# First shift and scale columns in two loads, tiles 0 and 1 one by one, small inputs on ScalarE's queue

## The chip, the cores and the metric

The kernel runs on one core of a Trainium2 chip. The metric is the device time of one execution in microseconds (us); lower is better. Before the change it is 2581.41 us, the median of three runs.

## What is computed

One layer of a backbone with gated recurrences, for 512 latent tokens x and 256 context tokens, model width D = 2048, all in fp32. The part that matters here is its beginning:

```
mod   = silu(c) @ w_mod + b_mod           # mod_c: the same with c_ctx
sh1, sc1, ... = split(mod, 6)
h  = rmsnorm(x, g_norm1)   * (1 + sc1)  + sh1
hc = rmsnorm(ctx, g_norm1) * (1 + csc1) + csh1
z  = h @ w_in                             # likewise hc @ w_in: the heads' inputs
```

`rmsnorm` divides by the root of the mean square over the 2048 channels, so no h exists before all of x has been seen. The scans, the output projection, the feed-forward part and the final norm follow; the change leaves them as they are.

## The kernel before

x stands transposed, channels on partitions, as 16 channel tiles `xl0` to `xl15` of 128 channels by 512 tokens. ctx stands as `xc`, 16 tiles of 128 by 256. Tiles go in pairs: pair kp is tiles 2kp and 2kp + 1.

**The sum of squares.** `stream_rstd` (called with "l" for latent, "c" for context) squares each tile on ScalarE (ACT), adds it on VectorE (DVE) into one tile `sq_l` or `sq_c`, and sums over the partitions with a product on TensorE (PE) against ones, `ss_l` or `ss_c`. `mean_rsqrt` makes 1/sqrt of it: Ln and Exp on ScalarE, and one Newton step on DVE; the result is `rstd`.

**The columns.** Scale (region 1) and shift (region 0) of a channel tile are columns `scol` and `shcol`. `mod_load` loads four 512 KB pieces of w_mod for one region and one pair; `mod_rows` multiplies them with the activated c and c_ctx (16 products of 256 columns, in the trace 32 records, output `ps_m`) and copies the result on ScalarE (`rows_m`); `mod_cols` turns the rows with two small products into columns, which DVE reads with the bias (`scol`, `shcol`). In the text m1_2 is the scale group of pair 2, m0_1 the shift group of pair 1. These groups and the sums of squares share two PSUM banks in turn ("psb").

**Modulation.** `modulate(n, ...)` multiplies the pair's tiles by rstd, applies the columns on DVE, casts to a high part `hTh` on ScalarE and subtracts on DVE to get a low part `hTl` (`hch`, `hcl` for ctx). Weights are split the same way (`hi_h`, `lo_h`, by `load_split`), and each product is made of three: high x high, high x low, low x high.

**Projection of the first two heads.** `project_first` works along the channel pairs. Head 0 keeps six banks a0_0 to a0_5 in PSUM over all pairs (g = 0, 1: 512 columns; 2, 3: 256 columns; 4, 5: the context, 384 columns). Head 1 has too few banks left: its groups a1_kp_g are made pair by pair (`early_group`), and ScalarE or DVE adds them to sums in SBUF (`e0_g`). The products of pair 0 begin with head 1's first two banks (`early_pair`).

**What sets the order.** While `pinned` is set, PE takes its instructions in the order in which they are written; ScalarE and DVE have a static order from the scheduler, in which `high_priority` moves instructions ahead. All large loads go through SyncE's queue (SP) in the order written. In the trace PE's products read `out<-in` with L95 as their line, since a helper records them all; `a` stands for all banks of both heads.

Of the kernel before, what the change touches and what calls it, by code (L numbers as in the profile page):

```python
# [11 lines left out]
F32 = mybir.dt.float32  # L12
# [57 lines left out]
def block_kernel(ctx: ExitStack, tc: tile.TileContext, a: dict, out: bass.AP):  # L70
# [14 lines left out]
    def add(o, x, y):  # L85
        V.tensor_tensor(out=o, in0=x, in1=y, op=ALU.add)  # L86

    def split(hi, lo, x):
        S.copy(hi, x)  # L89
        return V.tensor_tensor(out=lo, in0=x, in1=hi.bitcast(F32), op=ALU.subtract).ins  # L90
# [66 lines left out]
    fillers = []  # L157
    rate, credit = [0], [0]

    def load_split(src, name, n=2, w=512):  # L160
        raw = wraw.tile([P, n, w], F32, name=f"raw_{name}", tag="raw")
        hi = whi.tile([P, n, w], F32R, name=f"hi_{name}", tag="hi")
        lo = wlo.tile([P, n, w], F32R, name=f"lo_{name}", tag="lo")
        nc.sync.dma_start(raw, src)
        with tc.high_priority():
            split(hi, lo, raw)
# [55 lines left out]

    def mod_rows(region, n, raws):

        bank = psb(f"ps_m{region}_{n}")
        ps = bank[:, 0:256]
# [4 lines left out]
        rows = tmp.tile([P, 256], F32, name=f"rows_m{region}_{n}", tag="rows")  # L231
        with tc.high_priority():
            S.copy(rows, ps)
        return bank, rows

    def mod_cols(region, n, bank, rows):
# [4 lines left out]
        with tc.high_priority():  # L241
            for b in range(2):
                k = 2 * n + b
                if region == 1:
                    V.tensor_scalar(out=scol[:, k, :], in0=pc[:, b, :], scalar1=bp1[:, k : k + 1],
                                    scalar2=gn1[:, k : k + 1], op0=ALU.add, op1=ALU.mult)
                else:
                    V.tensor_scalar(out=shcol[:, k, :], in0=pc[:, b, :], scalar1=bmod[:, k : k + 1],
                                    scalar2=None, op0=ALU.add)

# [51 lines left out]

    def project_chunk(kp, wh, wl, o, g, first=0, last=KT - 1):

        ks = list(enumerate((2 * kp, 2 * kp + 1)))
        if g < 2:
# [39 lines left out]

    def early_pair(w, sums):

        (wh, wl), ps = w, [psb(f"a1_0_{g}", BANKS[g]) for g in range(2)]
        for n, (ws, xs) in enumerate(((wh, hx[0]), (wl, hx[0]), (wh, hx[1]))):  # L350
            for k in range(2):
                for g in range(2):
                    mm(ps[g], ws[:, k, P * g : P * g + P], xs[k], start=(n == 0 and k == 0), stop=(n == 2 and k == 1))
        for g in range(2):
            sums[g] = actp.tile(list(BANKS[g]), F32, name=f"e0_{g}", tag=f"ah{KT - 4 + g}")
            with tc.high_priority():
                S.activation(sums[g], ps[g], AF.Copy, scale=SCALE if g == 0 else 1.0)

    def project_first():

        banks = [acc(f"a0_{g}", BANKS[g]) for g in range(6)]
        sums = [None] * 4 + [accp.tile([P, DK + DV], F32, name=f"e0_{4 + j}", tag=f"sum{j}") for j in range(CJ)]
        stream_rstd(xl, rl, "l", T)
# [3 lines left out]
        for j in range(KT // 2):  # L367
            nc.sync.dma_start(xcp[j], a["ctxT"][j])
        raws = {r: mod_load(r, 1) for r in (1, 0)}
        with tc.high_priority():  # L370
            ins = modulate(0, "x")
# [10 lines left out]
        with tc.high_priority(), tc.issue_after(ins):  # L382
# [10 lines left out]
        w1 = load_split(a["w_heads"][1, 1], f"h1_1")  # L393
        for r in (1, 0):
            raws[r] = mod_load(r, 2)
        nc.sync.dma_start(cst[:, 0:C_SA], a["consts"][:, 0:C_SA])
        project_chunk(0, *w0, banks[4], 4)
        rows = mod_rows(1, 2, raws[1])
        project_chunk(0, *w0, banks[5], 5)
        mod_cols(1, 2, *rows)  # L400
        for kp in range(1, KP):
            for g in range(6):
                if g == 5 and kp + 1 < KP:
                    rows = mod_rows(0, kp + 1, raws[0])
                ins = early_group(kp, g, w1, sums)
                if g == 2:
                    with tc.issue_after(ins):
                        w0 = load_split(a["w_heads"][0, kp], f"h0_{kp}")
                    if kp + 2 < KP:
                        raws[1] = mod_load(1, kp + 2)  # L410
            if kp + 1 < KP:
                mod_cols(0, kp + 1, *rows)
                with tc.issue_after(ins):
                    modulate(kp + 1, "xc")
            for g in range(6):
                if g == 3 and kp + 2 < KP:
# [788 lines left out]
def arrange(x, c, ctx, c_ctx, w_mod, b_mod, g_norm1, g_norm2, w_in, gla_w_lr, gla_b_lr, mlstm_b_gate,  # L1205
# [61 lines left out]
```

## Time and profile before

| | before |
|---|---|
| median of three runs | 2581.41 us (2580.79 to 2584.02) |
| profiled execution, its own time | 2580.88 us |
| its span, first to last instruction | 2579.2 us |
| PE busy | 2536.5 us, 98% of the span |
| DVE busy | 1399.1 us, 54% |
| ACT busy | 789.9 us, 31% |
| first projection product starts | 30.70 us |

The profile is of one execution. Times in the views count from the first instruction. A timeline row gives start, duration, engine, line and operation, and in square brackets the idle time of its engine ahead of it with what ended it. Products overlap a little, so a row's duration is longer than the distance to the next start. PEclk is TensorE's granted clock as a share of 2.4 GHz.

### The profile page before, as it was taken

The numbers are of one execution on the slowest core, as the hardware profiler recorded it, in microseconds if no ns is written. First come the engines' busy times: TensorE is split into PE (matmuls) and PEld (weight loads), VectorE is DVE, ScalarE is ACT, GpSimd is POOL, SyncE is SP. The second block draws the span as 40 slices with busy tenths as digits, with TensorE's granted clock in tenths as the row PEclk, the third lists the DMA queues.
The fourth block names the chain that finished last, engine by engine and source line by source line (L and its number), as shares of the span: only waits on it lengthen the run. The fifth ranks groups of instructions, "written<-read, shape, count | busy, mean of one in ns | idle before, by whom it ended". The sixth has DMA issues, their size and how long they took to land.

```text
span 2579.2 us, 31641 instructions
## 1 busy us (share of the span) xinstructions
PE 2536.5 (98%) x12944; PEld 2128.3 (83%) x12944; DVE 1399.1 (54%) x2071; ACT 789.9 (31%) x1177; POOL 28.2 (1%) x53
## 2 busy tenths in 40 slices
PE   6999999999999999999999999999999999999998
PEld 4887899888887888888888888888888888888887
DVE  6556755554445677449866336533653265336534
ACT  4224543322223233224323123312331233123332
POOL 0000000000000000000000000000000000000001
PEclk9999999999999999999999999999999999999999
DMA  9740011132334777424722222322232223222323
GB/s 383 270 160 34 33 42 50 42 123 99 115 115 165 259 254 238 147 87 159 269 98 91 97 98 98 98 98 94 94 98 98 98 98 97 94 95 89 104 94 107
DMA packets 96345, 321.35 MB, mean 125 GB/s; under 512 B 10884, under 2 KB 15304, under 8 KB 96200
## 3 DMA queue, kind: packets, MB, share of 16 engines
q1 hardware_dynamic: 95112, 318.29, 35.7%
q8 instruction: 101, 1.65, 0.3%
q10 hardware_dynamic: 1088, 1.05, 0.1%
q14 instruction: 44, 0.36, 0.0%
HBM read 315.10 MB, written 4.19 MB: 124 GB/s over the span
## 4 chain that ended last, share of the span: by engine, by line
PE 93%; DVE 3%; DMA 2%; ACT 1%; issue 1%; SPq 0%; DVEq 0%; ACTq 0%
PE ug L95 18%; PE uv L95 18%; PE dn L95 17%; PE a L95 17%; PE wo L95 7%; PE ga L95 6%; PE po L95 4%; DMA raw_m<-in_w_mod 2%; PE ps_m L95 1%; PE sl L95 1%; PE dl L95 1%; DVE sum_m L264 1%; PE cst L95 0%; DVE sq_l L86 0%; PE gm L95 0%
## 5 line engine op out<-in xcount | busy, mean ns | idle before, releaser
L95 PE MATMUL uv<-h2h,hi_uv 128*128 128x512 f32 x688 | 267.7, 389 | 0.0
L95 PE MATMUL uv<-h2l,hi_uv 128*128 128x512 f32 x688 | 267.6, 389 | 0.0
L95 PE MATMUL uv<-h2h,lo_uv 128*128 128x512 f32 x688 | 267.6, 389 | 0.0
L95 PE MATMUL ug<-h2h,hi_ug 128*128 128x512 f32 x688 | 267.4, 390 | 0.0
L95 PE MATMUL ug<-h2l,hi_ug 128*128 128x512 f32 x688 | 266.6, 389 | 0.0
L95 PE MATMUL ug<-h2h,lo_ug 128*128 128x512 f32 x688 | 266.6, 389 | 0.0
L95 PE MATMUL dn<-gh,hi_d 128*128 128x512 f32 x644 | 250.5, 389 | 0.0
L95 PE MATMUL dn<-gl,hi_d 128*128 128x512 f32 x644 | 250.5, 389 | 0.0
L95 PE MATMUL dn<-gh,lo_d 128*128 128x512 f32 x644 | 250.5, 389 | 0.0
L1098 DVE SCALAR_TENSOR_TENSOR cv<-pad,cwt,cv 128x512 f32<-128x512 f32 x344 | 237.9, 753 | 8.5 <-ACT cv L1096 7.2
L90 DVE TENSOR_TENSOR lo_ug<-raw_ug,hi_ug 128x1024 fp32r<-128x1024 f32 (+1 forms) x88 | 105.5, 1199 | 248.9 <-ACT hi_ug L89 248.9
L264 DVE SCALAR_TENSOR_TENSOR sum_m<-raw_m,csil,sum_m 128x512 f32<-128x512 f32 x240 | 180.1, 751 | 56.6 <-DMA raw_m<-in_w_mod 51.1
L90 DVE TENSOR_TENSOR lo_uv<-raw_uv,hi_uv 128x1024 fp32r<-128x1024 f32 (+1 forms) x88 | 105.6, 1200 | 174.8 <-ACT hi_uv L89 174.4
L90 DVE TENSOR_TENSOR lo_d<-raw_d,hi_d 128x1024 fp32r<-128x1024 f32 x82 | 98.8, 1205 | 169.7 <-ACT hi_d L89 168.8
L89 ACT CAST hi_ug<-raw_ug 128x1024 fp32r<-128x1024 f32 (+1 forms) x88 | 90.9, 1033 | 304.9 <-PE ug L95 225.3
L89 ACT CAST hi_uv<-raw_uv 128x1024 fp32r<-128x1024 f32 (+1 forms) x88 | 90.9, 1033 | 261.8 <-PE uv L95 186.5
L89 ACT CAST hi_d<-raw_d 128x1024 fp32r<-128x1024 f32 x82 | 85.1, 1038 | 278.6 <-PE dn L95 224.3
L95 PEld LDWEIGHTS ug<-h2h,hi_ug 128*128 128x128 f32 x688 | 129.1, 188 | 27.4 <-issue 0.8
L95 PEld LDWEIGHTS ug<-h2h,lo_ug 128*128 128x128 f32 x688 | 129.2, 188 | 27.0
L95 PEld LDWEIGHTS uv<-h2h,hi_uv 128*128 128x128 f32 x688 | 129.2, 188 | 26.9
L95 PEld LDWEIGHTS uv<-h2l,hi_uv 128*128 128x128 f32 x688 | 129.2, 188 | 26.7
L95 PEld LDWEIGHTS uv<-h2h,lo_uv 128*128 128x128 f32 x688 | 129.2, 188 | 26.7
(307 smaller groups left out, 4945.2 us busy)
## 6 DMA issues: line engine op xcount, KB each, us to landing
raw_m<-in_w_mod SPq DMA_DIRECT2D x192, 512.0 KB, 4.9
raw_ug<-in_w_up SPq DMA_DIRECT2D x80, 512.0 KB, 3.2
raw_uv<-in_w_up SPq DMA_DIRECT2D x80, 512.0 KB, 3.3
raw_d<-in_w_down SPq DMA_DIRECT2D x79, 512.0 KB, 3.3
raw_h<-in_w_heads SPq DMA_DIRECT2D x64, 512.0 KB, 3.3
raw_ga<-in_w_gates SPq DMA_DIRECT2D x32, 512.0 KB, 3.9
raw_wo<-in_w_out SPq DMA_DIRECT2D x32, 512.0 KB, 3.2
xl<-in_xT SPq DMA_DIRECT2D x16, 256.0 KB, 5.1
```

The source lines that it names most:

```text
L89: S.copy(hi, x)
L90: return V.tensor_tensor(out=lo, in0=x, in1=hi.bitcast(F32), op=ALU.subtract).ins
L95: ins = PE.matmul(*args, **kw)
L264: V.scalar_tensor_tensor(out=parts[0], in0=x, scalar=ck, in1=parts[0], op0=ALU.mult, op1=ALU.add)
L1098: V.scalar_tensor_tensor(out=t3, in0=src, scalar=w, in1=t3, op0=ALU.mult, op1=ALU.add)
```

## The change

Three small inputs are loaded through ScalarE's queue and no longer through SP's. For tiles 0 and 1 the w_mod pieces are loaded one tile at a time, each region in two loads of 512 KB (`mod_load_half`), from a new arrangement w_mod0 of the array, and the products are 128 columns wide; tile 0's come ahead of the weights, tile 1's behind them. Tile 0 is modulated and used before tile 1's columns exist. `modulate_x` writes `hTh` directly on ScalarE with the columns as scale and bias. The first products belong to head 0; those of head 1's first two banks follow, tile by tile. Products whose result nothing reads (`unread`) stand on PE: one as each of xl2 to xl15 lands, two behind each half group of tile 0, and ten ahead of the first projection product (before: eight that read rstd). The context's sum of squares comes right behind tile 1's products, ahead of a1_0_2 and a1_0_3. Columns of pair 1 follow later, and those of pair 2 (m1_2, m0_2) lie within pair 1's products. From pair 2 on the order is as before.

```diff
-    nc.sync.dma_start(cv, a["cvec"])
-    nc.sync.dma_start(cst[:, C_SA:], a["consts"][:, C_SA:])
-    nc.sync.dma_start(cols, a["cols"])
+    nc.scalar.dma_start(cv, a["cvec"])
+    nc.scalar.dma_start(cst[:, C_SA:], a["consts"][:, C_SA:])
+    nc.scalar.dma_start(cols, a["cols"])
...
+    def mod_load_half(region, k):
+        raws = []
+        for i in range(2):
+            pl = wraw if (region, k, i) == (0, 1, 1) else mraw
+            raws.append(pl.tile([P, 8, P], F32, name=f"raw_m{region}h{k}_{i}", tag="raw"))
+            nc.sync.dma_start(raws[-1], a["w_mod0"][k, region, i])
+        return raws
+    def half_rows(region, k, raws):
+        return mod_rows(region, f"h{k}", [r[:, 4 * i : 4 * i + 4, :] for r in raws for i in range(2)], P)
+    def half_col(region, k, bank, rows):
+        pc = bank[:, 256:258]
+        mm(pc, rows, cc(C_SA, 2), start=True, stop=True)
+        with tc.high_priority():
+            mod_col(region, k, pc)
+    def unread(o, x, n=1):
+        for _ in range(n):
+            mm(o[:, 0 : x.shape[1]], ones, x, start=True, stop=True)
...
+    def modulate_x(k):
+        if k:
+            mul(xl[k], xl[k], rl)
+        for part, t in zip(hx, "hl"):
+            part.append(acttile(k, t, f"hT{t}{k}"))
+        sk, bk = scol[:, k, 0:1], shcol[:, k, 0:1]
+        ins = S.activation(hx[0][k], xl[k], AF.Identity, scale=sk, bias=bk).ins
+        V.tensor_scalar(out=xl[k], in0=xl[k], scalar1=sk, scalar2=bk, op0=ALU.mult, op1=ALU.add)
+        return ins, V.tensor_tensor(out=hx[1][k], in0=xl[k], in1=hx[0][k].bitcast(F32), op=ALU.subtract).ins
...
     def project_first():
+        for k in range(2, KT):
+            unread(spare, xl[k][:, 0:256])
         stream_rstd(xl, rl, "l", T)
-        for r in (1, 0):
-            mod_cols(r, 0, *mod_rows(r, 0, mod_load(r, 0)))
-        w1, w0 = (load_split(a["w_heads"][h, 0], f"h{h}_0") for h in (1, 0))
+        halves = {(r, 0): mod_load_half(r, 0) for r in (1, 0)}
+        w0 = load_split(a["w_heads"][0, 0], "h0_0")
+        w1 = load_split(a["w_heads"][1, 0], "h1_0")
+        halves.update({(r, 1): mod_load_half(r, 1) for r in (1, 0)})
...
+        for r in (1, 0):
+            rows = half_rows(r, 0, halves[r, 0])
+            unread(spare, xl[KT - 1][:, 0:P], 2)
+            half_col(r, 0, *rows)
+        unread(spare, xl[KT - 1][:, 0:P], 10)
...
-        for _ in range(8):
-            mm(banks[5][:, 0:P], ones, rl[:, 0:P], start=True, stop=True)
-        early_pair(w1, sums)
-        for g in range(2, 4):
-            early_group(0, g, w1, sums)
-        project_chunk(0, *w0, banks[0], 0)
-        rows = mod_rows(1, 1, raws[1])
-        project_chunk(0, *w0, banks[1], 1)
-        mod_cols(1, 1, *rows)
+        for k in range(2):
+            with tc.high_priority(), tc.issue_after(ready[0]), tc.issue_after(ready[1]):
+                ins = modulate_x(k)
+            first_part(w0, banks, k, ((0, 0), (1, 0)), range(2))
+            if k == 0:
+                rows = half_rows(1, 1, halves[1, 1])
+            first_part(w0, banks, k, ((0, 0), (1, 0)), range(2, 4))
+            if k == 0:
+                half_col(1, 1, *rows)
+                rows = half_rows(0, 1, halves[0, 1])
+            first_part(w0, banks, k, ((0, 1),), range(4))
+            if k == 0:
+                half_col(0, 1, *rows)
+            for g in range(2):
+                project_chunk(0, *w1, pair[g], g, 0, 1, only=(k,))
...
             stream_rstd([x.rearrange("p a b -> p (a b)") for x in xcp], rc, "c", TC)
             ins = modulate(0, "c")
-        for g in range(2, 4):
-            project_chunk(0, *w0, banks[g], g)
+        early_group(0, 2, w1, sums)
+        rows = mod_rows(1, 1, raws[1])
+        early_group(0, 3, w1, sums)
+        mod_cols(1, 1, *rows)
+        project_chunk(0, *w0, banks[4], 4)
+        project_chunk(0, *w0, banks[5], 5)
         rows = mod_rows(0, 1, raws[0])
         early_group(0, 4, w1, sums)
         mod_cols(0, 1, *rows)
...
-        project_chunk(0, *w0, banks[4], 4)
-        rows = mod_rows(1, 2, raws[1])
-        project_chunk(0, *w0, banks[5], 5)
-        mod_cols(1, 2, *rows)
```

`first_part` issues, for one tile and some of head 0's banks, the products of the named parts (high or low weights by high or low h).

**Where PE meets the context's sum.** On PE, ahead of and behind `ss_c`, before (a row is line, operation, output and inputs; the numbers at the end of a name only count):

```order
L95 MATMUL a0_1_175<-hTl0_341,hi_h0_0_308 128x512
L95 MATMUL a0_1_175<-hTh0_340,lo_h0_0_309 128x512
L95 MATMUL a0_1_175<-hTh1_345,hi_h0_0_308 128x512
L95 MATMUL a0_1_175<-hTl1_346,hi_h0_0_308 128x512
L95 MATMUL a0_1_175<-hTh1_345,lo_h0_0_309 128x512
L95 MATMUL ps_m1_1_411<-cst_58,rows_m1_1_428 128x2 x2
L95 MATMUL ss_c_463<-sq_c_440,cst_58 128x256 x2
L95 MATMUL a0_2_176<-hi_h0_0_308,hTh0_340 128x256
```

The same place after the change:

```order
L97 MATMUL a1_0_0_174<-hTh1_434,hi_h1_0_268 128x512
L97 MATMUL a1_0_0_174<-hTl1_435,hi_h1_0_268 128x512
L97 MATMUL a1_0_0_174<-hTh1_434,lo_h1_0_269 128x512
L97 MATMUL a1_0_1_175<-hTh1_434,hi_h1_0_268 128x512
L97 MATMUL a1_0_1_175<-hTl1_435,hi_h1_0_268 128x512
L97 MATMUL a1_0_1_175<-hTh1_434,lo_h1_0_269 128x512
L97 MATMUL ss_c_492<-sq_c_469,cst_58 128x256 x2
L97 MATMUL a1_0_2_515<-hi_h1_0_268,hTh0_362 128x256
```

Before, a1_0_2, a1_0_3 and the products of m1_1 stand ahead of `ss_c`; after, they stand behind it.

**The additions of the context on DVE.** DVE ahead of the first additions of `sq_c`, before:

```order
L504 TENSOR_SCALAR xl1_126<-xl1_126,scol_119,shcol_120 128x512
L90 TENSOR_TENSOR lo_h1_0_303<-raw_h1_0_301,hi_h1_0_302 128x1024
L90 TENSOR_TENSOR hTl0_341<-xl0_125,hTh0_340 128x512
L90 TENSOR_TENSOR hTl1_346<-xl1_126,hTh1_345 128x512
L90 TENSOR_TENSOR lo_h0_0_309<-raw_h0_0_307,hi_h0_0_308 128x1024
L86 TENSOR_TENSOR sq_c_440<-sq_c_440,sq_c1_442 128x512
```

And after:

```order
L92 TENSOR_TENSOR lo_h1_0_269<-raw_h1_0_267,hi_h1_0_268 128x1024
L569 TENSOR_TENSOR hTl0_363<-xl0_125,hTh0_362 128x512
L274 TENSOR_SCALAR scol_119<-ps_m1_h1_371,bp1_118,cols_59 128x2
L277 TENSOR_SCALAR shcol_120<-ps_m0_h1_400,cols_59 128x2
L568 TENSOR_SCALAR xl1_126<-xl1_126,scol_119,shcol_120 128x512
L569 TENSOR_TENSOR hTl1_435<-xl1_126,hTh1_434 128x512
L86 TENSOR_TENSOR sq_c_469<-sq_c_469,sq_c1_471 128x512
```

Tile 1's columns, which come out of PE's products (`ps_m1_h1`, `ps_m0_h1`), now stand ahead of the additions, with the multiply-add and `hTl1` that need them.

**What PE has ahead of pair 1.** PE up to the first products of pair 1 (`a1_1_0`), before:

```order
L95 MATMUL ps_m1_2_602<-raw_m1_2_2_583,cact_115 32x256 x4
L95 MATMUL ps_m1_2_602<-raw_m1_2_3_585,cact_115 32x256 x4
L95 MATMUL a0_5_179<-hi_h0_0_308,hch0_477 128x384
L95 MATMUL a0_5_179<-lo_h0_0_309,hch0_477 128x384
L95 MATMUL a0_5_179<-hi_h0_0_308,hcl0_478 128x384
L95 MATMUL a0_5_179<-hi_h0_0_308,hch1_482 128x384
L95 MATMUL a0_5_179<-lo_h0_0_309,hch1_482 128x384
L95 MATMUL a0_5_179<-hi_h0_0_308,hcl1_483 128x384
L95 MATMUL ps_m1_2_602<-cst_58,rows_m1_2_619 128x2 x2
L95 MATMUL a1_1_0_631<-hTh2_554,hi_h1_1_574 128x512
L95 MATMUL a1_1_0_631<-hTl2_555,hi_h1_1_574 128x512
```

And after:

```order
L97 MATMUL ps_m0_1_580<-cst_58,rows_m0_1_597 128x2 x2
L97 MATMUL a1_0_5_611<-hi_h1_0_268,hch0_506 128x384
L97 MATMUL a1_0_5_611<-lo_h1_0_269,hch0_506 128x384
L97 MATMUL a1_0_5_611<-hi_h1_0_268,hcl0_507 128x384
L97 MATMUL a1_0_5_611<-hi_h1_0_268,hch1_511 128x384
L97 MATMUL a1_0_5_611<-lo_h1_0_269,hch1_511 128x384
L97 MATMUL a1_0_5_611<-hi_h1_0_268,hcl1_512 128x384
L97 MATMUL a1_1_0_658<-hTh2_624,hi_h1_1_644 128x512
L97 MATMUL a1_1_0_658<-hTl2_625,hi_h1_1_644 128x512
L97 MATMUL a1_1_0_658<-hTh2_624,lo_h1_1_645 128x512
L97 MATMUL a1_1_0_658<-hTh3_634,hi_h1_1_644 128x512
```

Before, the column products of m0_1 stood ahead of a1_0_5, and a0_4, m1_2's products and a0_5 came between that and pair 1; after, a1_0_5 alone is left there.

## Rows read from the trace of the kernel before

**Rows 1.** The page's first part: each engine's busy time, share and instructions.

```profile
PE 2536.5 (98%) x12944; PEld 2128.3 (83%) x12944; DVE 1399.1 (54%) x2071; ACT 789.9 (31%) x1177; POOL 28.2 (1%) x53
```

**Rows 2.** Windows: stretch, length, PE busy (records), PEclk, DMA share, GB/s.

```profile
30.70:76.30 45.60, 44.90 (x380) 1.00 0.99 388
```

**Rows 3.** Timeline of PE, 19 to 31 us.

```profile
19.55 2.08 PE L95 MATMUL ss_l<-sq_l,cst 128*128 128x512 f32 x2 [19.55 <-DVE sq_l L86]
21.56 3.42 PE L95 MATMUL ps_m<-raw_m,cact 128*32 128x256 f32 x32
...
26.02 1.93 PE L95 MATMUL ps_m<-raw_m,cact 128*32 128x256 f32 x32
...
28.91 2.03 PE L95 MATMUL a<-rstd,cst 128*128 128x128 f32 x16
30.70 1.22 PE L95 MATMUL a<-hTh,hi_h 128*128 128x512 f32 x4
```

**Rows 4.** Timeline of PE, 37 us: products of 256 and 512 columns.

```profile
37.06 0.28 PE L95 MATMUL a<-hi_h,hTl 128*128 128x256 f32 x1
37.18 0.40 PE L95 MATMUL a<-hTh,hi_h 128*128 128x512 f32 x1
37.41 0.40 PE L95 MATMUL a<-hTl,hi_h 128*128 128x512 f32 x1
```

**Rows 5.** Timeline of SP's queue, 0 to 3 us.

```profile
0.80 0.39 SPq L460 DMA_DIRECT2D cv<-in_cvec  x1
...
2.18 0.91 SPq L467 DMA_DIRECT2D xl<-in_xT  x2
```

**Rows 6.** Timeline of DVE and ACT, 8 to 26 us.

```profile
8.46 11.04 DVE L86 TENSOR_TENSOR sq_l<-sq_l,sq_l 128x512 f32<-128x512 f32 x14 [1.28 <-ACT sq_l L484]
...
25.23 0.69 DVE L83 TENSOR_TENSOR xl<-xl,rstd 128x512 f32<-128x512 f32 x1
...
21.67 0.69 ACT L149 ACTIVATE scr_l<-ss_l,eps 128x512 f32<-128x512 f32 x1 [3.10 <-PE ss_l L95]
```

**Rows 7.** Timeline of DVE and PE around the context's sum.

```profile
37.09 2.29 DVE L86 TENSOR_TENSOR sq_c<-sq_c,sq_c 128x512 f32<-128x512 f32 x3 [0.20 <-ACT sq_c L484]
...
42.01 0.50 PE L95 MATMUL ps_m<-cst,rows_m 128*128 128x2 f32 x4
42.37 1.11 PE L95 MATMUL ss_c<-sq_c,cst 128*128 128x256 f32 x4
```

**Rows 8.** Timeline of DVE, 49 to 55 us: modulation of pair 1.

```profile
49.96 0.34 DVE L248 TENSOR_SCALAR shcol<-ps_m,cols 128x2 f32<-128x2 f32 x2
...
52.88 1.23 DVE L90 TENSOR_TENSOR lo_h<-raw_h,hi_h 128x1024 fp32r<-128x1024 f32 x1 [0.41 <-ACT hi_h L89]
...
54.35 0.69 DVE L90 TENSOR_TENSOR hTl<-xl,hTh 128x512 fp32r<-128x512 f32 x1
```

**Rows 9.** Like operations elsewhere: instructions of tiles h2h, out; timeline at 642 us.

```profile
L1054 ACT ACTIVATE h2h<-h,mod x16: 714/723/727, 1155.0 to 1179.4; 128x512 fp32r<-128x512 f32 x16
...
L1176 ACTq DMA_DIRECT2D out<-o x4: 378/404/826, 2572.0 to 2574.5; - x4
...
642.75 0.43 PE L270 MATMUL mr<-sum_m,cst 128*32 128x128 f32 x8
643.10 0.50 PE L95 MATMUL a<-hTh,hi_h 128*128 128x512 f32 x1
```

**Rows 10.** PE's timeline and windows around two idle times.

```profile
789.90 0.40 PE L95 MATMUL ga<-hTh,lo_ga 128*128 128x512 f32 x1
793.30 1.23 PE L95 MATMUL po<-c,qs 128*128 128x258 f32 x2 [3.00 <-DVE ed L83]
...
792.60:799.40 6.80, 6.09 (x15) 0.50 0.43 141
...
543.33 0.70 PE L95 MATMUL po<-c,qs 128*128 128x258 f32 x2 [1.67 <-DVE ed L83]
...
544.00:547.40 3.40, 3.40 (x17) 1.00 0.83 267
```

More of the change, by code (lines that the diff above doesn't have):

```diff
@@ L86, in add @@
         V.tensor_tensor(out=o, in0=x, in1=y, op=ALU.add)
+    cast = [None]
     def split(hi, lo, x):
-        S.copy(hi, x)
+        cast[0] = S.copy(hi, x).ins
         return V.tensor_tensor(out=lo, in0=x, in1=hi.bitcast(F32), op=ALU.subtract).ins
@@ L158, in block_kernel @@
     rate, credit = [0], [0]
+    parted = [None]
     def load_split(src, name, n=2, w=512):
@@ L165, in load_split @@
         with tc.high_priority():
-            split(hi, lo, raw)
+            parted[0] = split(hi, lo, raw)
         credit[0] += rate[0]
@@ L230, in mod_rows @@
                    start=(q == 0), stop=(q == 3), skip_group_check=True)
-        rows = tmp.tile([P, 256], F32, name=f"rows_m{region}_{n}", tag="rows")
+        rows = tmp.tile([P, w], F32, name=f"rows_m{region}_{n}", tag="rows")
         with tc.high_priority():
@@ L242, in mod_cols, with mod_col @@
             for b in range(2):
[L243 to L249, printed above, removed]
+                mod_col(region, 2 * n + b, pc[:, b, :])
+    def mod_col(region, k, pc):
+        if region == 1:
+            V.tensor_scalar(out=scol[:, k, :], in0=pc, scalar1=bp1[:, k : k + 1],
+                            scalar2=gn1[:, k : k + 1], op0=ALU.add, op1=ALU.mult)
+        else:
+            V.tensor_scalar(out=shcol[:, k, :], in0=pc, scalar1=bmod[:, k : k + 1],
+                            scalar2=None, op0=ALU.add)
     def mod_chunk(region, n, kp, parts):
@@ L300, in sum_tile, with project_chunk @@
         return accp.tile([P, T], F32, name=f"sum{i}_{name}", tag=f"sum{i}")
-    def project_chunk(kp, wh, wl, o, g, first=0, last=KT - 1):
-        ks = list(enumerate((2 * kp, 2 * kp + 1)))
+    def project_chunk(kp, wh, wl, o, g, first=0, last=KT - 1, only=(0, 1)):
+        ks = [(kk, 2 * kp + kk) for kk in only]
         if g < 2:
@@ L345, in early_group, with first_part @@
                 return V.scalar_tensor_tensor(out=o, in0=ps, scalar=scale, in1=old, op0=ALU.mult, op1=ALU.add).ins
[L347 to L353, printed above, removed]
+    def first_part(w, banks, k, parts, gs):
+        for g in gs:
+            for n, (i, j) in enumerate(parts):
+                start = k == 0 and n == 0 and len(parts) == 2
+                if g < 2:
+                    mm(banks[g], w[i][:, k, P * g : P * g + P], hx[j][k], start=start, stop=False)
+                else:
+                    for b in range(2):
+                        js = slice(P * (2 * g - 4 + b), P * (2 * g - 3 + b))
+                        mm(banks[g][:, b, :], hx[j][k][:, js], w[i][:, k, 256:], start=start and b == 0, stop=False,
+                           skip_group_check=True)
@@ new lines, in project_first @@
+    def project_first():
+        pair = [acc(f"a1_0_{g}", BANKS[g]) for g in range(2)]
+        banks = [acc(f"a0_{g}", BANKS[g]) for g in range(4)]
+        sums = [None] * 4 + [accp.tile([P, DK + DV], F32, name=f"e0_{4 + j}", tag=f"sum{j}") for j in range(CJ)]
+        spare = banks[3].rearrange("p a b -> p (a b)")
+        for k in range(2, KT):
+            unread(spare, xl[k][:, 0:256])
+        stream_rstd(xl, rl, "l", T)
+        halves = {(r, 0): mod_load_half(r, 0) for r in (1, 0)}
+        w0 = load_split(a["w_heads"][0, 0], "h0_0")
+        ready = cast[0], parted[0]
+        w1 = load_split(a["w_heads"][1, 0], "h1_0")
+        halves.update({(r, 1): mod_load_half(r, 1) for r in (1, 0)})
+        for j in range(KT // 2):
+            nc.sync.dma_start(xcp[j], a["ctxT"][j])
+        raws = {r: mod_load(r, 1) for r in (1, 0)}
+        for r in (1, 0):
[3 more added lines that the diff above has]
+        unread(spare, xl[KT - 1][:, 0:P], 10)
+        with tc.high_priority():
+            mul(xl[0], xl[0], rl)
+        for k in range(2):
[13 more added lines that the diff above has]
+                project_chunk(0, *w1, pair[g], g, 0, 1, only=(k,))
@@ L356, in early_pair @@
             with tc.high_priority():
[L357 to L363, printed above, removed]
-        for r in (1, 0):
-            mod_cols(r, 0, *mod_rows(r, 0, mod_load(r, 0)))
-        w1, w0 = (load_split(a["w_heads"][h, 0], f"h{h}_0") for h in (1, 0))
[L367 to L371, printed above, removed]
-        for _ in range(8):
-            mm(banks[5][:, 0:P], ones, rl[:, 0:P], start=True, stop=True)
-        early_pair(w1, sums)
-        for g in range(2, 4):
-            early_group(0, g, w1, sums)
-        project_chunk(0, *w0, banks[0], 0)
-        rows = mod_rows(1, 1, raws[1])
-        project_chunk(0, *w0, banks[1], 1)
-        mod_cols(1, 1, *rows)
-        with tc.high_priority(), tc.issue_after(ins):
+                S.activation(sums[g], pair[g], AF.Copy, scale=SCALE if g == 0 else 1.0)
+        banks += [acc(f"a0_{g}", BANKS[g]) for g in range(4, 6)]
+        with tc.high_priority(), tc.issue_after(ins[0]), tc.issue_after(ins[1]):
             stream_rstd([x.rearrange("p a b -> p (a b)") for x in xcp], rc, "c", TC)
             ins = modulate(0, "c")
-        for g in range(2, 4):
-            project_chunk(0, *w0, banks[g], g)
+        early_group(0, 2, w1, sums)
[4 more added lines that the diff above has]
+        project_chunk(0, *w0, banks[5], 5)
         rows = mod_rows(0, 1, raws[0])
```

32 lines of the change are left out of this document (23 added, 9 removed).

## Prediction

> **What bounds the kernel now.** The page's first part shows TensorE (PE) busy for 98% of the span [rows 1]. The windows show what the start is worth: from the first projection product at 30.70 us to the first product of channel pair 2 at 76.30 us PE is busy 44.90 of 45.60 us [rows 2]. In such a stream a product that starts later moves everything behind it. So only two things count: when the first projection product can start, and what PE then loses (idle time or added work) up to the place where both programs run alike. That place is the start of pair 2.
>
> The PE timeline of the start shows a chain without slack [rows 3]: ss_l, the sum over partitions, begins when DVE's 15 additions end (19.55); then scale products, copy, columns, shift products, columns, the filler products on rstd (28.91), and the first projection product. The same rows show a clock step. The 32 products of the scale group took 3.42 us, the 32 equal ones of the shift group 1.93 us, and ss_l (one product of 512 columns in two passes) 2.08 us: the first two ran at TensorE's low level, 1.2 GHz, the third at 2.4. (The clock column reads 1.00 before any product has run, so durations say more there.)
>
> **The start, term by term.** *Small loads on ScalarE's queue.* The first load of x is issued at 2.18, behind three small ones that begin at 0.80 [rows 5]; without them all sixteen move up by 1.38 us. A load of the output, issued on ScalarE's queue, took 0.40 us to issue [rows 9], so three take 1.2, beside ScalarE's first wait for data. The additions are one unbroken run on DVE, 14 in 11.04 us [rows 6], fed by loads and squares that come in step. I expect the whole move: last addition at 19.50 − 1.38 = 18.1. Bounds: 1.4 (all) and 0 (ScalarE late by its three issues, or arrival of data the limit).
>
> *After ss_l.* With a full clock ss_l takes half of 2.08, so it ends near 19.2. From ScalarE's Ln on it (21.67) to the end of the multiplication of tile 0 by rstd (25.23 + 0.69) is 4.25 us [rows 6], which gives 23.5. One scale column (0.28) now stands inside that run on DVE, one shift column (about 0.3) behind it, then ScalarE writes hTh0 straight from the columns. The same kind of activation took 0.72 [rows 9]: ready at 24.9.
>
> *PE meanwhile.* A half group has 32 records of 128 columns. Bounds: half of the 1.93 that 32 records of 256 columns took at full clock [rows 3] is 0.97; four times the 0.35 from one start to the next of eight records of 128 columns [rows 9] is 1.40. I take 1.16. Column products cost 0.36 (42.01 to 42.37) [rows 7]. A filler product of 128 columns costs (30.70 − 28.91)/8 = 0.22 [rows 3]. So: 19.2 + 1.16 + two fillers 0.44 + 0.36 (the copy lies beside the fillers) = 21.2; the shift half the same, 23.1; then ten fillers, 2.2: first projection product at 25.4, and 24.9 is covered by it. Against 30.70 that is **−5.3**. Behind them the stream is as full as before, less the 0.70 us that it stood idle [rows 2], which I put down to head 1's first banks: they waited for evictions that the new order doesn't have so early: **−0.7**.
>
> **What is given back.**
>
> *Tile 1's halves in the stream.* Before, pair 0's groups ran while nothing else could. Now tile 1's two halves and their columns lie among projection products: 2 × (1.16 + 0.36) = **+3.0** (2.7 to 3.5). The full groups of pairs 1 and 2 only change place (m1_2 goes from ahead of pair 1 to behind a1_1_1) and cost nothing by number, up to 76 us.
>
> *The context sum.* ss_c stood behind most of head 1's and head 0's first banks; its last three additions ended at 37.09 + 2.29 = 39.38 and PE came at 42.37: no wait [rows 7]. Now it stands ahead of a1_0_2 and a1_0_3, which with m1_1 are worth PE time. PE reaches it after 24 products of 512 columns (0.232 each, start to start) and 24 of 256 (0.12) [rows 4], 8.4 us, and the 3.0: 25.4 + 11.4 = 36.8. On DVE the seven additions stand behind hTl1. PE ends tile 1's shift products and hTl0's about 5.5 us after 25.4, at 30.9; column product, column, ScalarE's hTh1 (0.72), DVE's multiply-add and hTl1 bring it to 33.4. Seven additions at 11.04/14 = 0.79 [rows 6] are 5.5: 38.9, and 0.1 to PE. 39.0 − 36.8: **+2.2** (1.5 to 3). The squares on ScalarE are behind hTh1 as well.
>
> *Before pair 1.* From the shift columns of m0_1 (49.96) to the end of hTl3 (54.35 + 0.69) DVE and ScalarE needed 5.08 us [rows 8]; the same instructions are in that stretch after the change (lo_h1_1 now ahead of hTl2). Before, PE had a1_0_5, a0_4, m1_2 and a0_5 for that time. Now only a1_0_5 is left, six products of 384 columns, 0.176 each by interpolation [rows 4], 1.05 us, and four products of a1_1_0 that need no hTl3, 0.93. With 0.4 us from column product to column: 5.08 + 0.4 − 1.05 − 0.93 = **+3.5**, in several pieces (bank of a1_0_5, hTh2 and hTl2 behind lo_h1_1, hTh3, hTl3). Bounds: 3.0 without the 0.41 that DVE waited for a cast in that block, 4.4 if those four products fit nowhere.
>
> Sum at full clock: −5.3 − 0.7 + 3.0 + 2.2 + 3.5 = **+2.7**.
>
> **The clock.** Where PE stood idle for 3.00 us, 790.30 to 793.30, the next 6.8 us ran at a granted clock of 0.50; where it stood for 1.67 us ahead of 543.33 the following stretch reads 1.00 [rows 10]. After the change PE has one 0.24 us product as each x tile lands, then nothing from the last landing (about 14.8) to ss_l at 18.1, 3.3 us. By the row at 793.30 ss_l starts at the low level, and what follows it until the clock is back runs at half speed. Bounds: 0 (ss_l at full clock), and +2.5 (all of ss_l, both halves and the fillers up to about 24.6 at half speed, as before up to 26.02, less what hides under the 4.25 us of DVE). ss_l alone costs 1.0. I take **+1.6**, nearer the row that shows the fall. Here the Trainium skill has a rule that speaks against the change: "TensorE: Matmul & The Clock Gate", section "HAM oscillation — how this bites in real kernels", says that a wait between bursts throttles the engine again, so that the next burst starts cold. The rows at 793.30 agree and the ones at 543.33 don't; by the rule alone the start would lose the whole 2.5, and each of the two new stalls a further spell. The trace shows both outcomes.
>
> Total: +4.3 on the profiled execution's 2580.88 (span 2579.2 and 1.68 around it), which lies 0.5 under the median of the runs shown: **2585.2 us**. What can be told from no change is 0.2%, 5.2 us.
>
> **Rivals.**
>
> *A further spell at low clock (slower).* The idle 2.2 us ahead of ss_c lies between the 1.67 that cost nothing and the 3.00 that cost a spell; the pieces before pair 1 add 3.5 within some 5 us. One spell like 792.60 to 799.40, 6.8 us at 0.50, takes 3.4 us of work: 2585.2 + 3.4 = 2588.6. It decides as soon as all losses by clock pass 2.5 us (2.7 + 2.5 = 5.2). For it: both new stalls are longer in sum than the one that cost nothing. Against: around both PE works at full rate. Also the full 2.5 at the start would just pass that bound. Chance 0.35.
>
> *The head start survives.* If DVE's additions for the context end by 36.8, and DVE's block at pair 1 is done earlier (the scheduler puts rstd multiplications ahead), then −5.3 − 0.7 + 3.0 = −3.0, 2577.9. For it: before, the additions were done 3 us ahead of PE; against: they stand behind hTl1 in DVE's written order, and 5.5 us of DVE work can't shrink. Chance 0.10. For a gain beyond 0.2% the halves in the stream would have to be hidden too; with a longer head start from the ScalarE queue I give that 0.07.
>
> *The start is no earlier than the data.* If the arrival of x sets the pace and the additions end at 19.5 as before, +1.4: 2586.6. For it: every addition needs a tile that has landed. Against: the additions follow each other without a gap from 8.46 on, so DVE's and ScalarE's rate sets their end, not the data. Chance 0.06.
>
> **How the numbers follow.** Forecast (all new waits, and at most 2.5 us lost by clock): 0.42. Range: the low end takes the surviving head start's upper part and the lower bounds of halves and waits (2.7 + 1.5 + 3.0 − 6.0 = +1.2) with no loss by clock, and then leaves a margin to 2578.5; the high end takes a further spell, 2589.5. Forecast's own range: 2582.1 to 2586.1. Faster by over 0.2%: 0.07; within: 0.55; slower: 0.38 (the further spell, and part of the third rival).
>
> **What would show it.** Right: SP's first x load near 0.8; last addition near 18.1; first projection product near 25.4; ss_c with 2 to 2.5 us of idle behind DVE's sq_c; PE idle 3 to 4 us in pieces between a1_0_4 and a1_1_3, released by hTl2, hTh3, hTl3; pair 2's first product near 79 to 80.7 and a constant difference from there on. Wrong: if products of one shape take twice as long in a stretch after 36 us, the clock fell there and the first rival holds; if ss_c has no idle time the second does; if the last addition ends after 19 the third does; and if the two traces part again after pair 2, the whole method (one offset passed through) is wrong.

## The result, and the profile after

The changed kernel takes 2590.33 us (median of 9 runs, 2584.81 to 2595.02); the kernel before, beside it on the same chip, 2581.18 (2576.95 to 2584.02). The ratio is 1.0033, 95% interval 1.0025 to 1.0042: slower by 6.5 to 10.8 us. The forecast was 2585.2, its range ended at 2589.5. The profiled execution has a span of 2590.1 us, 10.9 more than before.

The page's first part shows PE busier than before, and by more than the added work:

```profile
span 2590.1 us, 31854 instructions
PE 2553.5 (99%) x13048; PEld 2140.6 (83%) x13048; DVE 1400.1 (54%) x2071; ACT 790.4 (31%) x1179; POOL 28.9 (1%) x53
```

PE has 17.0 us more busy time than in [rows 1]; that is where to look: products that take longer, or new ones. PE's timeline of the stretch that the prediction walked through, with the idle time ahead of a row in brackets:

```profile
17.93 2.07 PE L97 MATMUL ss_l<-sq_l,cst 128*128 128x512 f32 x2 [2.82 <-DVE sq_l L86]
19.93 1.94 PE L97 MATMUL ps_m_h<-raw_m1h,cact 128*32 128x128 f32 x32
...
25.11 2.48 PE L97 MATMUL a<-xl,cst 128*128 128x128 f32 x20
27.35 0.48 PE L97 MATMUL a<-hTh,hi_h 128*128 128x512 f32 x1
28.45 1.08 PE L97 MATMUL ps_m_h<-raw_m1h,cact 128*32 128x128 f32 x32
...
41.62 2.05 PE L97 MATMUL ss_c<-sq_c,cst 128*128 128x256 f32 x4 [2.87 <-DVE sq_c L86]
46.16 2.61 PE L97 MATMUL ps_m<-raw_m,cact 128*32 128x256 f32 x32
...
55.88 0.50 PE L97 MATMUL ps_m<-cst,rows_m 128*128 128x2 f32 x4
56.98 0.41 PE L97 MATMUL a<-hi_h,hch 128*128 128x384 f32 x1 [0.60 <-DVE shcol L277]
59.41 0.50 PE L97 MATMUL a<-hTl,hi_h 128*128 128x512 f32 x1 [0.89 <-DVE hTl L92]
60.85 0.50 PE L97 MATMUL a<-hTh,hi_h 128*128 128x512 f32 x1 [0.71 <-ACT hTh L91]
61.58 0.80 PE L97 MATMUL a<-hTl,hi_h 128*128 128x512 f32 x1 [0.23 <-DVE hTl L92]
...
69.36 0.38 PE L97 MATMUL a<-hi_h,hTh 128*128 128x256 f32 x1 [0.45 <-DVE e L374]
...
85.74 0.48 PE L97 MATMUL a<-hTh,hi_h 128*128 128x512 f32 x1
```

The waits are where they were forecast, and so are their releasers. What is new is in the durations: ss_l takes 2.07 us as before, the first half group 1.94 and a later one of the same shape 1.08; ss_c takes 2.05, where it took 1.11 [rows 7]. Pair 2 starts at 85.74, before at 76.30: +9.4. The windows of the same kernel (length, PE busy, PEclk, DMA share, GB/s) say why:

```profile
18.00:20.00 2.00, 2.00 (x6) 0.50 1.02 416
24.00:26.00 2.00, 2.00 (x34) 1.00 1.02 414
42.00:44.00 2.00, 2.00 (x7) 0.50 0.95 383
48.00:50.00 2.00, 2.00 (x27) 1.00 0.85 262
62.00:64.00 2.00, 2.00 (x6) 0.50 0.75 305
66.00:68.00 2.00, 2.00 (x29) 1.00 0.54 156
```

Behind each of the three idle places PE runs at 1.2 GHz for some microseconds, busy all the while and half as fast. The other engines' timelines show the chain at the start and the additions in front of ss_c:

```profile
0.81 4.25 SPq L532 DMA_DIRECT2D xl<-in_xT  x8
6.04 11.83 DVE L86 TENSOR_TENSOR sq_l<-sq_l,sq_l 128x512 f32<-128x512 f32 x15
25.77 0.81 ACT L567 ACTIVATE hTh<-xl,shcol,scol 128x512 fp32r<-128x512 f32 x1
34.77 0.69 DVE L569 TENSOR_TENSOR hTl<-xl,hTh 128x512 fp32r<-128x512 f32 x1
40.78 0.69 DVE L86 TENSOR_TENSOR sq_c<-sq_c,sq_c 128x512 f32<-128x512 f32 x1 [0.31 <-ACT sq_c L549]
```

SP issues x from 0.81 on (2.18 before [rows 5]), the additions end at 17.87 (19.50 before), hTl1 at 35.46, and the last of the context's additions at 41.47.

### The profile page after: what moved, and what is told of

The parts are those of the page before. It is cut to its first block, busy times and chain, and to the rows that moved or that the text cites. A ratio compares the mean times of both kernels' runs of the same rounds, so it can differ in the third digit from the quotient of the medians.

```text
span 2590.1 us, 31854 instructions
## 1 busy us (share of the span) xinstructions
PE 2553.5 (99%) x13048; PEld 2140.6 (83%) x13048; DVE 1400.1 (54%) x2071; ACT 790.4 (31%) x1179; POOL 28.9 (1%) x53
## 4 chain that ended last, share of the span: by engine, by line
PE 89%; DVE 6%; DMA 3%; issue 1%; ACT 1%; DVEq 0%; ACTq 0%
PE dn L97 17%; PE ug L97 16%; PE uv L97 16%; PE a L97 16%; PE wo L97 7%; PE ga L97 6%; PE po L97 3%; DMA raw_m<-in_w_mod 3%; PE sl L97 1%; PE dl L97 1%; PE ps_m L97 1%; DVE sum_m L293 1%; DVE cv L1173 1%; DVE h2l L1130 0%; DVE sq_l L86 0%
```

## Experiments

Two theories stood against each other. **A, the clock:** the waits and the added work cost what was summed at full clock (+2.7), and the rest is time at half clock behind the new idle times. **B, order and work:** the low clock is hidden under DVE's and ScalarE's chains and landing data, and the loss is in the waits and the added groups. The mark in every run is the start of pair 2, from where on the order is the same in all kernels; before it stands at 76.30. Behind the mark the times of single profiles still scatter: from it to the end they need between 2497.7 and 2507.6 us (before 2502.9, after 2504.4), so a profile's own time says little about what stands ahead of the mark.

**Idle time ahead of ss_l filled (e1_fill_ssl).**

```diff
         for k in range(2, KT):
             unread(spare, xl[k][:, 0:256])
+        unread(spare, xl[KT - 1][:, 0:256], 6)
```

> The changed kernel with six more unread products of 256 columns between the last landing of x and ss_l, so that PE no longer stands idle for 2.82 us ahead of ss_l. Theory A (the clock: each of the three new idle times lowers the granted clock, and what is then done at half speed is lost in full): ss_l takes about 1.0 us in place of 2.07, the half groups run at full speed, the first projection product starts at about 25.4 in place of 27.35, and pair 2 starts about 2 us earlier than its 85.74 (some 83.7). Theory B (the waits alone: the clock falls are hidden under DVE's and ScalarE's chains and under landing data): the first projection product may come earlier, but ss_c stays near 41.6 and pair 2 within 0.5 us of 85.74.

Ratio 1.0023 (1.0014 to 1.0033). PE's timeline:

```profile
18.59 1.12 PE L97 MATMUL ss_l<-sq_l,cst 128*128 128x512 f32 x2 [0.44 <-DVE sq_l L86]
19.65 1.08 PE L97 MATMUL ps_m_h<-raw_m1h,cact 128*32 128x128 f32 x32
25.57 0.48 PE L97 MATMUL a<-hTh,hi_h 128*128 128x512 f32 x1
39.84 1.64 PE L97 MATMUL ss_c<-sq_c,cst 128*128 128x256 f32 x4 [2.92 <-DVE sq_c L86]
```

ss_l starts 0.66 us later than in the changed kernel, and the first projection product all the same 1.8 us earlier; ss_c moves by the same 1.8. From ss_l to the first projection product it is 6.98 us here and 9.42 in the profile after. So the low clock at the start isn't hidden: B is wrong there. Pair 2 starts at 81.41, 4.3 earlier and not 2: in this execution the clock was also low for a shorter time at ss_c (1.64) and stayed up before pair 1, which theory A had not foreseen.

**Idle time ahead of ss_c filled (e2_fill_ssc).**

```diff
+        if name == "c":
+            unread(ps, xl[KT - 1][:, 0:256], 6)
         for i in range(0, T, n):
             mm(ps, ones, tot[:, i : i + n], start=(i == 0), stop=(i + n == T))
```

> The changed kernel with six unread products of 256 columns just ahead of ss_c, in ss_c's own bank, so that PE is busy while it waits for DVE's additions; the wait itself stays. Theory A: ss_c still starts at about 41.6, but then takes 1.1 and not 2.05 us, a1_0_2 and m1_1 run at full speed, and pair 2 starts about 2.7 us earlier, near 83. Theory B: 85.7 within 0.5, since DVE's chain for the context sets the pace behind ss_c.

Ratio 1.0015 (1.0006 to 1.0025). ss_c starts as before the edit, 41.52, and takes 1.13:

```profile
17.73 2.08 PE L97 MATMUL ss_l<-sq_l,cst 128*128 128x512 f32 x2 [2.40 <-DVE sq_l L86]
38.56 2.75 PE L97 MATMUL ss_c<-xl,cst 128*128 128x256 f32 x12
41.52 1.13 PE L97 MATMUL ss_c<-sq_c,cst 128*128 128x256 f32 x4 [0.21 <-DVE sq_c L86]
```

With ss_c at the same place and at full clock, the column products of m0_1 come earlier and pair 2 starts at 81.58, 4.2 earlier. B, which said 85.7, is wrong here too: the low clock behind ss_c was not hidden. Of the 4.2, 2.7 belong to ss_c; the rest is again that the clock stayed up before pair 1. That the fill is what kept the clock up at ss_c is not shown by this run: below, the same wait without a fill is also followed by full clock.

**Context additions earlier (e3_adds_early).**

```diff
-        with tc.high_priority(), tc.issue_after(ins[0]), tc.issue_after(ins[1]):
+        with tc.high_priority(), tc.issue_after(tile0[0]), tc.issue_after(tile0[1]):
             stream_rstd([x.rearrange("p a b -> p (a b)") for x in xcp], rc, "c", TC)
```

(`tile0` is what `modulate_x(0)` returned.)

> The changed kernel with the context's squares and additions allowed to start behind tile 0's modulation and not behind tile 1's, so that the additions lie among tile 1's instructions on DVE. Theory A: the wait at ss_c falls from 2.87 to about 1.5 us, too short for a fall of the clock, and pair 2 starts about 4 us earlier (1.3 of wait and 2.7 of clock), near 81.7. Theory B: only the 1.3 of the wait, near 84.4.

Ratio 1.0011 (0.9999 to 1.0022). The wait at ss_c falls to 1.34 us, ss_c takes 1.10, and pair 2 starts at 80.90, 4.8 earlier, where theory A had 4 and B 1.3. The sum is not a test of A by itself, since in this execution the clock was low for a shorter time at the start (first projection product at 26.63) and fell before pair 1.

**Pair 1's shift columns earlier (e4_pair1).**

```diff
-        early_group(0, 3, w1, sums)
         mod_cols(1, 1, *rows)
+        rows = mod_rows(0, 1, raws[0])
+        early_group(0, 3, w1, sums)
+        mod_cols(0, 1, *rows)
         project_chunk(0, *w0, banks[4], 4)
         project_chunk(0, *w0, banks[5], 5)
-        rows = mod_rows(0, 1, raws[0])
         early_group(0, 4, w1, sums)
-        mod_cols(0, 1, *rows)
```

> The changed kernel with the shift columns of pair 1 (m0_1) made ahead of a0_4, a0_5, a1_0_4 and a1_0_5 in PE's order, so that all four lie between these columns and pair 1, as three groups did before the change. Theory A: the idle pieces before and in a1_1_0 (2.43 us) almost vanish and with them the spell at half clock from about 61 to 64.6 (1.5 us of work): pair 2 starts about 3.5 to 4 us earlier, near 82. Theory B: 2.3 earlier, near 83.4, with the low clock still granted somewhere behind it or without effect.

Ratio 1.0010 (1.0000 to 1.0019). Pair 2 starts at 76.68, 9.1 earlier, and this was the surprise: the edit touches nothing ahead of 40 us, the idle times there are as before, yet the clock fell at neither.

```profile
17.67 1.12 PE L97 MATMUL ss_l<-sq_l,cst 128*128 128x512 f32 x2 [2.60 <-DVE sq_l L86]
24.65 0.48 PE L97 MATMUL a<-hTh,hi_h 128*128 128x512 f32 x1
38.93 1.10 PE L97 MATMUL ss_c<-sq_c,cst 128*128 128x256 f32 x4 [2.90 <-DVE sq_c L86]
```

So theory A had to be changed: an idle time of this size lowers the clock in some executions and not in others. Most of the 9.1 us is therefore luck of this execution; the gain of the order itself shows against the filled kernel below (78.75 to 76.68, 2.1 us).

**The changed kernel again (e8_after_again, e12_after_timed).** No edit.

> The changed kernel unchanged, a second profile. If a fall of the clock is fixed by the program, the same three stretches (from 17, from 41 and from 61 us) run at half clock and pair 2 starts at 85.7 again. If it depends on the execution, some of them run at full clock at the same idle times, and pair 2 starts between 79 and 86.

The second profile shows the same idle times, and full clock behind two of the three (the clock was low only for a part of the start):

```profile
17.78 1.12 PE L97 MATMUL ss_l<-sq_l,cst 128*128 128x512 f32 x2 [2.42 <-DVE sq_l L86]
18.83 1.90 PE L97 MATMUL ps_m_h<-raw_m1h,cact 128*32 128x128 f32 x32
26.11 0.48 PE L97 MATMUL a<-hTh,hi_h 128*128 128x512 f32 x1
40.38 1.10 PE L97 MATMUL ss_c<-sq_c,cst 128*128 128x256 f32 x4 [2.90 <-DVE sq_c L86]
51.89 0.50 PE L97 MATMUL ps_m<-cst,rows_m 128*128 128x2 f32 x4
80.38 0.48 PE L97 MATMUL a<-hTh,hi_h 128*128 128x512 f32 x1
```

The same program starts pair 2 at 80.38 in one execution and at 85.74 in another, and this one took 2581.30 us. The profiles of e1, e2 and e3 (81.41, 81.58, 80.90) lie between these two, so none of the three shows by its pair 2 alone what its edit did.

> The changed kernel itself, on the same chip and beside the same runs of the kernel before as the filled one. Theory A: 4 to 6 us above the filled one in the median, with a wider spread of its executions. Theory B: within 1.5 us of it.

A third profile has low clock at the start only (ss_l 2.08 behind 3.23 us of idle time, ss_c 1.10 behind 2.90) and pair 2 at 82.04. The ratio in this timing is 1.0017 (1.0008 to 1.0026), the median 2588.20 against 2583.09. Against the filled kernel beside it (next run) the changed one is 3.5 us slower in the median, where theory A had 4 to 6 and B 1.5 at most, and its executions spread no wider (10.3 us against 9.8), where A had a wider spread.

**All idle places filled, nothing else (e11_all_filled).** The edits of the first two runs, and four unread products ahead of a1_1_0:

```diff
         ps = psb(f"a1_{kp}_{g}", BANKS[g])
+        if (kp, g) == (1, 0):
+            unread(ps, xl[KT - 1][:, 0:256], 4)
```

> The changed kernel with its order and its waits as they are, and unread products of 256 columns in all three idle places: six ahead of ss_l, six ahead of ss_c, four ahead of a1_1_0. Nothing starts earlier by that except through the clock. Theory A (clock): no stretch between 17 and 80 us at half clock, pair 2 between 78.9 and 79.7 in the profile, and the ratio to the kernel before near 1.001 (2.6 to 3.4 us, the waits and the added work alone), against 1.0033 for the changed kernel. Theory B (order and added work make up the loss): ratio as for the changed kernel, 1.0025 to 1.004.

```profile
17.58 1.12 PE L97 MATMUL ss_l<-sq_l,cst 128*128 128x512 f32 x2
24.56 0.47 PE L97 MATMUL a<-hTh,hi_h 128*128 128x512 f32 x1
38.73 1.13 PE L97 MATMUL ss_c<-sq_c,cst 128*128 128x256 f32 x4 [0.21 <-DVE sq_c L86]
78.75 0.48 PE L97 MATMUL a<-hTh,hi_h 128*128 128x512 f32 x1
```

Pair 2 starts at 78.75, earlier than in all three profiles of the changed kernel, and no stretch from 15 us up to there is at half clock. That is +2.45 on the kernel before, with order, waits and added groups of the change: the sum at full clock. The ratio is 1.0008 (0.9999 to 1.0017), the median 2584.70, 3.5 us under the changed kernel beside it. The intervals of the two overlap at 1.0008 to 1.0017, so the times alone leave it open; the place of pair 2 is shown by the profiles alone. This profile also shows why times scatter behind the mark: its execution took 2587.09 us, that of the third profile of the changed kernel 2581.47, though pair 2 stands 3.3 us earlier here. Between 1170 and 1440 us PE waits 1.6 and 0.9 us for DVE's low parts of the feed-forward weights (`lo_uv`, `lo_ug`), and in the other execution not at all.

**All covered (e5_all_covered).** The fills of e1 and e2 and the order of e4 together.

> The changed kernel with the six unread products ahead of ss_l, the six ahead of ss_c, and pair 1's shift columns earlier, all three at once. Theory A (the clock makes up what the waits do not): no idle time over 1 us is left ahead of pair 1, no stretch between 17 and 80 us at half clock, pair 2 starts near 77.2 (0.9 behind before's 76.30: 5.3 us gained at the start less 3.0 for tile 1's halves and 2.9 for the wait at ss_c, which stays, filled), the time is 0.5 to 1.5 us above before, and the several runs of the kernel spread no more than before's. Theory B (order and added work make it up): pair 2 stays behind 80.

Pair 2 at 76.63, no half clock ahead of it; 2583.63 us, ratio 1.0003 (0.9994 to 1.0011): what the change lost is gone, and nothing is won.

**Parts of the change in the kernel before (e6_before_act_queue, e7_before_queue_fill).** The three loads on `nc.scalar` alone, and with fills:

```diff
+        for k in range(2, KT):
+            mm(banks[5][:, 0:256], ones, xl[k][:, 0:256], start=True, stop=True)
+        for _ in range(6):
+            mm(banks[5][:, 0:256], ones, xl[KT - 1][:, 0:256], start=True, stop=True)
         stream_rstd(xl, rl, "l", T)
```

> The kernel before with one part of the change alone: the three small inputs on ScalarE's queue. If the start is a chain without slack, the last addition ends 1.4 us earlier and pair 2 starts 1.0 to 1.4 us earlier, near 75. If the arrival of x or ScalarE's issues set the pace, nothing moves (76.3).

ss_l starts at 18.49, 1.06 earlier, and pair 2 at 75.48, 0.8 earlier; the ratio, 0.9992 (0.9983 to 1.0001), can't be told from no change.

> The kernel before with two parts of the change: small inputs on ScalarE's queue, and unread products of 256 columns as xl2 to xl15 land, with six more behind the last so that PE is busy up to ss_l. Order, columns in pairs, and everything behind ss_l as before. Theory A: ss_l takes 1.1 in place of 2.08, the scale group 1.9 in place of 3.42, pair 2 starts near 73.9 (2.4 earlier), and the time is 2 to 3 us below before. Theory B (the rest of the start, DVE's chain or landing data, hides the clock): as with the queue alone, about 75.

Pair 2 at 74.86, 1.4 earlier; ratio 0.9987 (0.9978 to 0.9996), 2578.60 against 2581.90 us: faster than both kernels. The other 1.0 us of the forecast 2.4 went into a new wait:

```profile
21.37 1.19 PE L95 MATMUL ps_m<-raw_m,cact 128*32 128x256 f32 x16
23.19 0.64 PE L95 MATMUL ps_m<-raw_m,cact 128*32 128x256 f32 x8 [0.63 <-DMA raw_m<-in_w_mod]
24.41 0.64 PE L95 MATMUL ps_m<-raw_m,cact 128*32 128x256 f32 x8 [0.59 <-DMA raw_m<-in_w_mod]
```

The shift products wait for the last loads of w_mod. Here theory B holds in part: once PE is fast enough, landing data is the limit, which before had been hidden behind products at half clock.

**A shorter chain (e9_ssc_later, e10_ssc_behind_m1).** The changed kernel with the fill of e1, eight fillers in place of ten, e3's edit, and PE's order behind tile 1 changed. The first, with a1_0_2 ahead of ss_c:

```diff
+        early_group(0, 2, w1, sums)
...
-        early_group(0, 2, w1, sums)
         rows = mod_rows(1, 1, raws[1])
         early_group(0, 3, w1, sums)
         mod_cols(1, 1, *rows)
+        rows0 = mod_rows(0, 1, raws[0])
+        mod_cols(0, 1, *rows0)
         project_chunk(0, *w0, banks[4], 4)
         project_chunk(0, *w0, banks[5], 5)
-        rows = mod_rows(0, 1, raws[0])
         early_group(0, 4, w1, sums)
-        mod_cols(0, 1, *rows)
```

> The changed kernel with all idle times shortened and not only filled: six unread products ahead of ss_l, eight fillers ahead of the first projection product in place of ten, context additions among tile 1's on DVE, ss_c behind a1_0_2, and both column groups of pair 1 (m1_1, m0_1) ahead of a0_4, a0_5 and a1_0_4. Theory A (head start kept where PE has no new wait): no idle time over 1 us between 17 and 75 us, no stretch at half clock, pair 2 near 74.2 (2.1 earlier than before), time 1.5 to 2.5 us below before. Theory B (tile 1's halves and landing data eat the head start whatever the order): pair 2 no earlier than 75.5.

Pair 2 at 74.90, ratio 0.9990 (0.9981 to 0.9999): just faster than before, 0.7 us short of the expectation. PE has two new waits, 1.05 and 0.49 us, for ScalarE's copies of the rows:

```profile
37.69 1.10 PE L97 MATMUL ss_c<-sq_c,cst 128*128 128x256 f32 x4
43.34 0.61 PE L97 MATMUL ps_m<-cst,rows_m 128*128 128x2 f32 x4 [1.05 <-ACT rows_m L260]
46.30 0.61 PE L97 MATMUL ps_m<-cst,rows_m 128*128 128x2 f32 x4 [0.49 <-ACT rows_m L260]
```

The second has m1_1's products ahead of ss_c and a1_0_2 behind it.

> As the run before, but m1_1's products ahead of ss_c and a1_0_2 behind it. Theory A: pair 2 near 73.9. If m1_1's last load lands too late for that place (38.5 us in the changed kernel), PE waits about 1 us there for the load and pair 2 comes near 74.8. Theory B: no earlier than 75.5.

Pair 2 at 75.62, as theory B had it here (no earlier than 75.5); ratio 0.9998 (0.9989 to 1.0008), no gain. PE waits for the loads (0.34 and 0.59 us), and a1_0_2 for the bank of ss_c, which DVE has yet to read:

```profile
37.41 0.64 PE L97 MATMUL ps_m<-raw_m,cact 128*32 128x256 f32 x8 [0.34 <-DMA raw_m<-in_w_mod]
38.65 0.64 PE L97 MATMUL ps_m<-raw_m,cact 128*32 128x256 f32 x8 [0.59 <-DMA raw_m<-in_w_mod]
39.21 1.13 PE L97 MATMUL ss_c<-sq_c,cst 128*128 128x256 f32 x4
41.37 0.39 PE L97 MATMUL a<-hi_h,hTh 128*128 128x256 f32 x1 [1.02 <-DVE var_c L152]
```

**All profiles counted.** Of the six profiles with the changed kernel's start and no further fill (after, e2, e3, e4, e8, e12) five have low clock behind the wait at ss_l; of the six with a fill there (e1, e5, e9, e10, e11, and e7 in the kernel before) none has. At ss_c, two of the five with the wait of about 2.9 us and no fill have it (after, e1), and none of the three with a fill (e2, e5, e11). Before pair 1, two of the six that keep this order without a fill have it (after, e3). So the fill at the start is shown to keep the clock up; at the other two places the counts are too small to tell it from chance.

## Why the prediction was wrong

The step that failed is **the clock**. The prediction gave it +1.6 us, all of it at the start, and put "a further spell at low clock" into a rival with a chance of 0.35 and a price of 3.4. In the profile after it cost 6.6 us. It can be told apart by place, between the same two products each time. From ss_l to the first projection product the profile after has 9.42 us, the filled kernel 6.98 (2.4). From ss_c to the column products of m0_1 it has 14.26 us, the second profile of the same kernel 11.51 (2.75). From there to pair 2 it has 29.86 against 28.49 (1.4). Nearly all of the rest of the way from 78.75 to 85.74 is that ss_l itself starts 0.35 later. In the other two profiles of the changed kernel the clock cost 1.35 (ss_l to the first projection product 8.33) and 2.3 (9.32), at the start alone. By the prediction's own sign, products of one shape that take twice as long behind 36 us, the first rival holds in the profile after, and it does not hold in the other two. So the direction of the rival was right, and its weight wrong in two ways: the start was priced at 1.6 where a full fall costs 2.4 (its bound of 2.5 was right), with the two later places taken as one chance; and the cost was thought of as fixed by the program, while it changes from one execution to the next. The mean of the three profiles, 3.4 us on top of the sum, would have given a total of about +6 in place of +4.3, and all three places together a high end above 2590.

The sum at full clock held, +2.7 forecast and +2.45 measured in the filled kernel (the three profiles of the changed kernel, less what the clock cost them, give +2.7 to +3.4), but by luck, since errors of its terms offset each other:

- **The start**, −5.3: 24.56 in the filled kernel against 30.70, −6.1. The fillers set the first product, as the prediction had it. The additions ended 2.0 us earlier there and 1.6 in the profile after, for the 1.4 forecast, and by another way than the loads of x moving up by 1.38: all 15 are now one run of 11.8 us, which begins when DVE is done with small operations on the three inputs, and these wait for the landing of `cols`. The run began at 5.70 in the filled kernel, 6.04 in the profile after and 6.70 in e1, and ss_l moved with it.
- **Idle time before**, −0.7: no product of head 1's first banks waits for an eviction any more, as forecast.
- **Tile 1's halves**, +3.0: a group took 1.00 from start to start (28.45 to 29.45) and its column 0.21, 2.4 for two. But from the first projection product to pair 2 PE worked 3.6 us more than before (second profile: 54.27 us less 5.8 of idle time, against 44.90 [rows 2]). Of the other 1.2, 0.7 lie in a1_1_0 and a1_1_1, whose 12 products took 2.85 us before (55.74 to 58.59) and, less their 1.84 us of idle time, 3.6 in the second profile (54.12 to 59.5): by the look of the timeline, a product beside a wait has no neighbour to overlap with. No run separates the rest.
- **The context's sum**, +2.2: 2.87 to 2.92 in every profile that has this wait. hTl1 ended at 35.46, the additions needed 6 us for the 5.5 forecast.
- **Before pair 1**, +3.5: 0.60 + 0.89 + 0.71 + 0.23 = 2.4 by the releasers that were named, and 0.45 ahead of a1_1_3, which waits for DVE's addition to head 1's sums: 2.9.

Added up as measured, −6.1 − 0.7 + 3.6 + 2.9 + 2.9 = +2.6.

The rule of the Trainium skill that was weighed, "TensorE: Matmul & The Clock Gate", section "HAM oscillation — how this bites in real kernels", says that a wait between bursts throttles the engine again. The profile after agrees with it at all three places. The second profile, with 2.90 us ahead of ss_c and 1.10 for ss_c, does not.

Two of the other rivals are out: the head start did not survive the wait at ss_c, and the additions ended at 17.87, not at 19.5. That one offset passes through behind pair 2 held for the profiles before and after to within 1.5 us: +9.4 at pair 2, +10.9 in the span. But three profiles of the one changed kernel differ by 6.7 us behind pair 2 (2504.4, 2499.2, 2497.7), by later falls of the clock and by other waits, so this agreement is in part luck.

What stays open is the size of the loss in the time. Two timings of the same change gave 1.0033 (1.0025 to 1.0042) and 1.0017 (1.0008 to 1.0026). The intervals just touch, and the forecast of +4.3 us lies outside the first and inside the second, which is 2.1 to 6.7 us. The executions of the second and third profile (2581.30 and 2581.47 us) are the fastest on record of the changed kernel, so these profiles are no fair sample of it; three are too few to say how often each place has a fall, or whether that depends on the chip. And no run shows that the falls ahead of pair 2 alone make up the loss in the medians.

## What to carry to other kernels

An edit that puts idle times of some microseconds ahead of full-rate matmul work has two prices, the wait and the slower clock behind it, and the second may be the larger (in the profile after 6.6 us, against 5.8 of new waits); before ordering work around such a wait, ask what else PE could do in it, products that nothing reads included. When the cost of a wait depends on the execution, one profile shows one draw: look at several profiles of the same kernel before reading a difference between two kernels into the edit. And a start that is made faster should be checked for the next limit: in the kernel before with a faster start it was the landing of w_mod.

## What the runs showed of the hardware that was not expected

The granted clock behind like idle times differs between executions of one program. Ahead of ss_c, 2.87 us of idle time was followed by half clock (ss_c 2.05), 2.90 twice by full clock in the same kernel (1.10), and 2.92 in e1 by a fall that came while ss_c ran (1.64). Ahead of ss_l, 2.40 us was followed by half clock in e2 (2.08), 2.60 by full clock in e4 (1.12).

An unread product of 256 columns in fp32 cost twice what the prediction had assumed: six of them are 12 records and took 2.75 us in e2, 0.46 each, against 0.12 from start to start for a product of 256 columns of the split weights [rows 4].
